# One buffer layout from the last output product to the end, half products two blocks a bank with split weights reused, and accumulators walked back and forth

## The chip, the cores and the metric

The kernel runs on one core of a Trainium2 chip. The metric is the device time of one execution in microseconds (us). Five engines run their own instruction streams: PE multiplies matrices (PEld is its loading of the stationary operand), DVE and ACT work on tiles, POOL here only starts DMAs, and SP starts most DMAs. Each of SP, POOL and ACT starts the DMAs that it is given in the order of its stream.

## The reference

One decoder layer on 512 tokens of width 2048, all in float32:

```python
mod = (silu(c) @ w_ada + b_ada).reshape(B, 6, D)
sh1, sc1, gt1, sh2, sc2, gt2 = ...
h = rmsnorm(x, g_norm_mix) * (1 + sc1) + sh1
proj = h @ w_in                      # q, k, v, xr, xg
mixed = concat([rmsnorm(stick_breaking_attention(q, k, v), g_attn_out),
                rmsnorm(rg_lru(conv(xr)) * gelu(xg), g_lru_out)])
x = x + gt1 * (mixed @ w_out)        # 2048 -> 2048
h = rmsnorm(x, g_norm_mlp) * (1 + sc2) + sh2
hid = square(relu(h @ w_mlp_in))     # 2048 -> 8192
x = x + gt2 * (hid @ w_mlp_out)      # 8192 -> 2048
return rmsnorm(x, g_norm_final)
```

## The kernel before

Channels lie on the partitions, tokens along the free axis; A and B are the first and the last 256 tokens. A float32 product is made of three matmuls (`mm3`): each operand is split into a rounded high half and the rest, and high x high, high x low and low x high are added in PSUM. For a weight tile ACT makes the high half (a copy, L207 or L911) and DVE the low half (a subtraction, `low`, L115).

The part that the change touches begins near 706 us, at the last of four output products (`mixed @ w_out`, 512 output channels each). It has these pieces:

- *The last output product*, `out_src(3)`: 16 blocks of 128 input channels; 256 tokens at a time (a half product of 192 matmuls of 128x256), half A and then half B. Each half loads and splits the 16 weight blocks of 256 KB afresh (tiles `wr`, `wh`, `wl`). `out_evac` adds the product to xT, which it loads then, and the sums of squares (L737). The result `x1` is stored to DRAM by 16 DMAs on SP.
- *Group 0 of mlp_in*, `in_src(0)`, again as two half products. Its operand comes from generators that run in the background, `norm3` with `prep_a` (tokens A) and `prep_b` (tokens B): a normalization, and the split of h. Every finished block is a tick, and a generator's `yield 1.0` says how many ticks it waits until its next piece. Between the halves the generator is drained and the stage changes.
- *Groups 1 to 15 of mlp_in*: 512 hidden channels each, by Strassen's seven products on 2 x 2 blocks (`strassen`). One of its steps, a set, loads one `raw` tile of weights (512 KB, L903), makes four sums of blocks on DVE (`ts`, L905, L912, L913), splits them (`w3` 768 columns and `w4` 1024 columns, L911 and L917) and issues 42 matmuls of 128x256 (L944 to L946). A group has eight sets and seven accumulators of one PSUM bank each, of eight banks. `combine` (L956 and on) makes four quarters of the seven; `sums()` made the sums of the activations ahead of group 1; `keep_parts` squares each group's result, splits it, forms four sums and stores it all to DRAM by POOL (`part`, `sum`, `p21`).
- *mlp_out*: 32 pairs (a pair is 256 hidden channels, half a group) times four groups n of 512 outputs, 124 sets by `strassen` and the rest, the last four pairs of n=3, as a plain product. Each set needs a pair's activations, five 256-KB loads on SP (`load_pair`, L985 and L988), whose sums are split three sets later (`arriving`, L994 and L115). 64 `a` tiles of 256 KB hold pairs, spills and results. The sets are walked in 18 parts (n, sets). When a part ends and its n is not finished, its seven accumulators are copied out (ACT L335 and DVE L337 in turn) and stored to DRAM by POOL (L1126); before a part whose n has been begun they are loaded by SP (`load_pre`, L1072, into seven `pre` tiles) and copied by ACT into PSUM (L934).
- *ada_late(GT2)*: the last modulation vector, 64 rows of 128x512 weights, each a load into `st` (256 KB, L1029) and a multiply with accumulation on DVE (L1040), one every 1.6 ticks in mlp_out.

Instructions are put in order by a scheduler that goes by the order of the program and by priorities (`tc.high_priority(offset=...)`: an offset moves the piece ahead by so much); after that each engine runs its list in order. Tiles come from rings: a tag with so many buffers; a writer waits until the last reader of the ring's oldest tile is done. Rings outside a stage last for the whole kernel (`BUFS`), those in `STAGES` lie over each other:

```python
    "front": {"x": 3, "tt": 5, "wr": 4, "wh": 3, "wl": 3, "n": 5},
    "mlp_in": {"raw": 3, "ts": 2, "w4": 6, "w3": 6},
    "mlp_out": {"raw": 3, "ts": 2, "w4": 4, "w3": 4, "pre": 7, "st": 2},
```

The walk of mlp_out:

```python
FROM = [0, 2, 3, 4]
parts = [(n, range(FROM[n])) for n in range(1, NO)]
parts += [(n, range(i + FROM[n], min(i + FROM[n] + 8, NP))) for i in range(0, NP, 8) for n in range(NO)]
```

Of the kernel before, what the change touches and what calls it, by code (L numbers as in the profile page):

```python
# [62 lines left out]
def hybrid_layer_kernel(  # L63
# [665 lines left out]
    def out_evac(bs, g, tok):  # L729
        for o in range(4):  # L730
# [6 lines left out]
            stt(out=t, in0=bs[o][:, tok], scalar=mod(GT1, k), in1=xr_[:, tok], op0=ALU.mult, op1=ALU.add)  # L737
# [558 lines left out]
```

## Time and profile before

| | |
|---|---|
| runs | 2165.39, 2159.66, 2163.75 us; median 2163.75 |
| profiled execution | 2159.86 us, span 2158.2 us |
| mean granted PE clock | 0.984 of full |
| PE busy in the span | 95% |
| DVE, ACT, POOL busy | 83%, 51%, 8% |
| DMA | 475.06 MB, mean 220 GB/s |

The profile is of one execution. A line number (L944) is that of the kernel before; a row gives line, engine, operation, tile written <- tile read, count and time. A wait is put down to the instruction whose end came last. PE's busy time counts modelled ends of matmuls, so a stretch where PE is busy all the time can still run at a slow clock; the granted clock stands beside it. What an engine other than PE waits for costs nothing by itself.

### The profile page before, as it was taken

How to read it: one execution, taken by the hardware profiler on the slowest of the kernel's cores; microseconds unless marked ns; L12 is line 12 of the kernel's file. 1: busy time of each engine (PE TensorE's matmuls, PEld its weight loads, DVE VectorE, ACT ScalarE, POOL GpSimd, SP SyncE). 2: the span in 40 equal slices, each digit the busy share in tenths (PEclk: the TensorE clock that was granted, in tenths of full speed). 3: DMA queues.
4: the chain of work that ended last, by engine and by line, in shares of the span. 5: the costliest groups of instructions: out<-in, count | busy, mean ns of one | idle time of the engine just before them, and what ended most of it. 6: DMA issues, size and time to landing. Idle time of an engine off the chain costs nothing.

```text
span 2158.2 us, 38620 instructions
## 1 busy us (share of the span) xinstructions
PE 2042.1 (95%) x14532; PEld 1907.9 (88%) x14532; DVE 1800.3 (83%) x3026; ACT 1107.8 (51%) x1657; POOL 180.2 (8%) x276
## 2 busy tenths in 40 slices
PE   7999999999999979999999999979999999999997
PEld 5779898778777868999999999979999999899996
DVE  6898775878888789998998988978888787877897
ACT  4433553885422575554544544554446445544452
POOL 0000000000000001121121121112001000100000
PEclk9999999999999999999999999989999999999999
DMA  8887644545779745565464555688768868777843
GB/s 287 281 292 239 202 146 139 164 146 181 234 254 317 252 143 179 165 199 167 150 202 157 167 186 165 191 324 304 259 217 316 304 232 287 254 274 260 309 144 113
DMA packets 225053, 475.06 MB, mean 220 GB/s; under 512 B 22497, under 2 KB 45153, under 8 KB 224866
## 3 DMA queue, kind: packets, MB, share of 16 engines
q1 hardware_dynamic: 201138, 400.63, 56.4%
q0 software_dynamic: 21280, 69.75, 8.9%
q8 instruction: 114, 1.87, 0.4%
q10 hardware_dynamic: 2448, 2.21, 0.3%
q14 instruction: 73, 0.60, 0.1%
HBM read 394.38 MB, written 78.12 MB: 219 GB/s over the span
## 4 chain that ended last, share of the span: by engine, by line
PE 35%; issue 26%; DMA 16%; DVE 13%; POOL 5%; ACT 3%; SPq 1%; POOLq 0%; DVEq 0%; ACTq 0%
DMA x<-in_w_adaT_dram 5%; PE ps_mm L222 3%; PE ps_mm L226 3%; PE ps_mm L225 3%; DVE w L115 3%; DMA raw<-in_w_mlp_out_dram 3%; POOL part L839 3%; PE ps_mm L946 3%; PE ps_mm L944 2%; PE ps_mm L945 2%; DMA st<-in_w_adaT_dram 2%; POOL sum L848 2%; DMA a<-sum 2%; PE ps_z L946 2%; PE ps_z L944 2%
## 5 line engine op out<-in xcount | busy, mean ns | idle before, releaser
L946 PE MATMUL ps_mm<-a,w 128*128 128x256 f32 x1704 | 483.4, 285 | 10.4 <-DVE w L115 9.9
L944 PE MATMUL ps_mm<-a,w 128*128 128x256 f32 x1704 | 482.9, 284 | 5.5 <-ACT w L911 5.3
L945 PE MATMUL ps_mm<-a,w 128*128 128x256 f32 x1704 | 481.2, 283 | 0.0
L911 ACT ACTIVATE w<-raw 128x768 fp32r<-128x768 f32 x244 | 205.5, 842 | 435.1 <-issue 124.9
L944 PE MATMUL ps_z<-a,w 128*128 128x256 f32 x1288 | 366.1, 284 | 19.9 <-ACT w L911 12.8
L946 PE MATMUL ps_z<-a,w 128*128 128x256 f32 x1288 | 366.5, 285 | 6.2 <-DVE w L115 6.2
L945 PE MATMUL ps_z<-a,w 128*128 128x256 f32 x1288 | 364.3, 283 | 0.0
L946 PEld LDWEIGHTS ps_mm<-a,w 128*128 128x128 f32 x1704 | 322.7, 190 | 15.4 <-DVE w L115 15.0
L944 PEld LDWEIGHTS ps_mm<-a,w 128*128 128x128 f32 x1704 | 324.0, 190 | 7.1 <-ACT w L911 6.1
L945 PEld LDWEIGHTS ps_mm<-a,w 128*128 128x128 f32 x1704 | 323.8, 190 | 0.0
L115 DVE TENSOR_TENSOR w<-raw,w 128x768 fp32r<-128x768 f32 (+1 forms) x262 | 244.5, 934 | 71.0 <-ACT w L911 67.0
L115 DVE TENSOR_TENSOR w<-ts,w 128x1024 fp32r<-128x1024 f32 x244 | 297.6, 1220 | 3.3 <-ACT w L917 3.1
L917 ACT ACTIVATE w<-ts 128x1024 fp32r<-128x1024 f32 x244 | 255.8, 1049 | 42.4 <-DVE ts L913 37.8
L944 PEld LDWEIGHTS ps_z<-a,w 128*128 128x128 f32 x1288 | 244.6, 190 | 22.3 <-ACT w L911 14.0
L946 PEld LDWEIGHTS ps_z<-a,w 128*128 128x128 f32 x1288 | 244.4, 190 | 9.6 <-DVE w L115 9.2
L181 DVE SCALAR_TENSOR_TENSOR x<-x,cb 128x1024 f32<-128x1024 f32 x160 | 195.5, 1227 | 64.0 <-DMA x<-in_w_adaT_dram 63.4
L945 PEld LDWEIGHTS ps_z<-a,w 128*128 128x128 f32 x1288 | 244.7, 190 | 0.0
L207 ACT ACTIVATE wh<-wr 128x512 fp32r<-128x512 f32 x232 | 142.9, 619 | 194.5 <-PE ps_mm L225 90.7
L905 DVE TENSOR_TENSOR ts<-raw 128x512 f32<-128x512 f32 x244 | 167.3, 687 | 69.7 <-DMA raw<-in_w_mlp_out_dram 59.5
L222 PE MATMUL ps_mm<-a,wh 128*128 128x512 f32 (+1 forms) x528 | 201.0, 381 | 8.7 <-DVE a L401 3.1
L226 PE MATMUL ps_mm<-a,wl 128*128 128x512 f32 (+1 forms) x528 | 200.0, 380 | 2.7 <-DVE wl L115 2.6
L115 DVE TENSOR_TENSOR wl<-wr,wh 128x512 fp32r<-128x512 f32 x232 | 158.5, 686 | 50.1 <-ACT wh L207 49.4
(293 smaller groups left out, 4134.7 us busy)
## 6 DMA issues: line engine op xcount, KB each, us to landing
x<-in_w_adaT_dram SPq DMA_DIRECT2D x160, 512.0 KB, 5.2
raw<-in_w_mlp_out_dram SPq DMA_DIRECT2D x124, 512.0 KB, 4.7
raw<-in_w_mlp_in_dram SPq DMA_DIRECT2D x120, 512.0 KB, 3.8
wr<-in_w_in_dram SPq DMA_DIRECT2D x160, 256.0 KB, 3.7
prod<-a POOLq DMA_DIRECT2D x98, 256.0 KB, 6.2
pre<-prod SPq DMA_DIRECT2D x98, 256.0 KB, 6.7
part<-a POOLq DMA_DIRECT2D x96, 256.0 KB, 3.6
a<-part SPq DMA_DIRECT2D x96, 256.0 KB, 6.6
```

What stands on the lines that cost most here:

```text
L115: tt(out=out, in0=full, in1=f32(high), op=ALU.subtract)
L181: stt(out=t, in0=t, scalar=1.0, in1=cb[q * n // 1024][:, o : o + n], op0=ALU.mult, op1=ALU.mult, accum_out=ga[:, q : q + 1],)
L207: act(h[:, :n], r[:, :n], AF.Copy)
L222: first = mm(out, wh, ah, start=start, stop=False, **kw)
L225: mm(out, wh, al, start=False, stop=False, **kw)
L226: mm(out, wl, ah, start=False, stop=stop, **kw)
L905: tt(out=t[:, : 2 * HT].rearrange("p (a b) -> p a b", a=2), in0=r[:, HT : 3 * HT].rearrange("p (a b) -> p a b", a=2), in1=r[:, q_(0)].unsq ...
L911: act(h, r[:, HT:], AF.Copy)
L917: act(h, t, AF.Copy)
L944: mm(out, wh[:, blk(i)], ah, start=st, stop=False, **kw)
L945: mm(out, wh[:, blk(i)], al, start=False, stop=False, **kw)
L946: mm(out, wl[:, blk(i)], ah, start=False, stop=j == js[-1], **kw)
```

## The change

1. *Stages.* `n` is a ring of the whole kernel; the stage `front` ends before the last output product, and one stage `mlp` follows to the end: `ts` 2, `raw` 3, `w4` 5, `w3` 6. The rings `pre` and `st` are gone.
2. *Half products.* `half_product` puts two blocks of outputs into one PSUM bank, so a half product takes two banks. It keeps the split weights of eight blocks of `out_src(3)` and ten of `in_src(0)` from half A and uses them in half B, which walks backwards. That is 18 loads and splits less. xT of the last product comes in two loads of 512 KB into `ts` tiles; the stores of x1 go from SP's queue to POOL's. `sums()` runs beside group 0 and group 1, in reverse order of j, and so do group 1's sets.
3. *ada_late* starts with group 2 of mlp_in, a row every 2.6 ticks, loaded three rows ahead: 47 rows run in mlp_in (tile `n`) and 17 in mlp_out (tile `a`).
4. *The last two groups* (pairs 28 to 31) stay in SBUF (`hold_parts`), and the order of the pairs is 28, 29, 0 to 3, 30, 31, 4 to 27. Each other pair is loaded four to seven sets before its first use and split two sets before it, by a table.
5. *The walk* goes back and forth: 13 parts, 9 spills and 9 reloads of seven accumulators instead of 14. Of a reload, five loads go out on POOL's queue at the part before, and two on ACT's queue at the border, all into `n` tiles.
6. *The tail's* kept weights lie in `w4` and `w3` instead of `w4` and `a`.

```diff
-    "front": {"x": 3, "tt": 5, "wr": 4, "wh": 3, "wl": 3, "n": 5},
-    "mlp_in": {"raw": 3, "ts": 2, "w4": 6, "w3": 6},
-    "mlp_out": {"raw": 3, "ts": 2, "w4": 4, "w3": 4, "pre": 7, "st": 2},
+    "front": {"x": 3, "tt": 5, "wr": 4, "wh": 3, "wl": 3},
+    "mlp": {"ts": 2, "raw": 3, "w4": 5, "w3": 6},
...
-    def norm3(tok, prep):
-        yield 1.8
-        rnorm([acc1], D, "o", tok, r2)
+    def norm3(tok, prep, ptag):
+        yield 5.0
+        rnorm([acc1], D, ptag, tok, r2)
...
+    def half_product(bs, src, operand, ks, held, keep={}):
+        for k in ks:
+            wh, wl = held[k] if k in held else weights(src(k), keep.get(k, "w4"))
+            if k in keep:
+                held[k] = wh, wl
+            ah, al = operand(k)
+            for o, out in enumerate(halves(bs)):
+                mm3(out, wh[:, blk(o)], wl[:, blk(o)], ah, al, k == ks[0] and o % 2 == 0, k == ks[-1], ...)
+            tick()
...
-    product(ba, out_src(3), mx, order, A)
-    out_evac(ba, 3, A)
...
+    stage("mlp")
+    half_product(b2, out_src(3), mixed_half(A), order, held, dict(zip(order[8:], ["w3"] * 3 + ["w4"] * 5)))
+    out_evac(halves(b2), 3, A, x3)
+    b2 = [bank("mm") for _ in range(2)]
+    for k in range(12):
+        nc.gpsimd.dma_start(x1D[k], x1[k])
+    bg.add(norm3(A, prep_a, "o"))
+    half_product(b2, out_src(3), mixed_half(B), order[::-1], held)
...
+    bg.add(norm3(B, prep_b, "z"), sums())
+    half_product(b2, in_src(0), h2_half(A), PAIRED, held, dict(zip(PAIRED[6:], ["w3"] * 3 + ["ts"] * 2 + ["w4"] * 5)))
...
+    half_product(b2, in_src(0), h2_half(B), BACK, held)
...
         if pre:
+            n, ts = pre
             with tc.high_priority(offset=SETE):
-                for b, t in zip(bs, pre):
+                for b, t in zip(bs, ts):
+                    act(b, t, AF.Copy)
+                for b, t in zip(bs[5:], load_pre(n, (5, 6), nc.scalar)):
                     act(b, t, AF.Copy)
...
+        if g == 2:
+            bg2.add(ada_late(GT2))
...
+        bg.add((keep_parts if g < NG - 2 else hold_parts)(g, *rs))
...
-    bg.drain()
-    stage("mlp_out")
+    parts = [
+        (0, range(8)), (1, range(8)), (2, range(8)), (3, range(16)), (2, range(8, 16)), (1, range(8, 16)), (0, range(8, 24)),
+        (1, range(16, 24)), (2, range(16, 24)), (3, range(16, 28)), (0, range(24, NP)), (1, range(24, NP)), (2, range(24, NP)),
+    ]
+    ORDER = [28, 29, 0, 1, 2, 3, 30, 31] + list(range(4, 28))
+            todo.setdefault(use - 7 - q % 8 + q % 8 * 3 // 2, []).append((load_pair, p))
+            todo.setdefault(use - 2, []).append((split_pair, p))
...
-    def load_pre(n):
-        ts = [T("pre") for _ in range(7)]
-        for t, d in zip(ts, prodD[n]):
-            nc.sync.dma_start(t, d)
+    def load_pre(n, js, queue=nc.gpsimd):
+        ts = [T("n") for _ in js]
+        for t, j in zip(ts, js):
+            queue.dma_start(t, prodD[n][j])
         return ts
...
-                return load_pre(left[0])
+                return left[0], load_pre(left[0], range(5))
...
-    tags = ["w4"] * 2 + ["a"] * 6
+    tags = ["w4"] * 3 + ["w3"] * 2 + ["w4"] * 2 + ["w3"]
```

How the instructions stand on the engines, at three places. First, SP at the start of the last output product, before (x is the last ada's tile, wr a weight block, n a block of xT, x_0 a block of x1 in DRAM):

```order
L177 DMA x_6273<-in_w_adaT_dram 128x1024
L199 DMA wr_6570<-in_w_out_dram 128x512
L199 DMA wr_6588<-in_w_out_dram 128x512
L199 DMA wr_6606<-in_w_out_dram 128x512
L735 DMA n_6476<-in_xT_dram 128x512
L199 DMA wr_6624<-in_w_out_dram 128x512
L735 DMA n_6482<-in_xT_dram 128x512
L735 DMA n_6488<-in_xT_dram 128x512
L199 DMA wr_6642<-in_w_out_dram 128x512
```

And in the changed kernel:

```order
L174 DMA x_6272<-in_w_adaT_dram 128x1024
L735 DMA n_6475<-in_xT_dram 128x512
L735 DMA n_6481<-in_xT_dram 128x512
L735 DMA n_6487<-in_xT_dram 128x512
L735 DMA n_6493<-in_xT_dram 128x512
L196 DMA raw_6579<-in_w_out_dram 128x512
L196 DMA raw_6596<-in_w_out_dram 128x512
L196 DMA raw_6613<-in_w_out_dram 128x512
L924 DMA ts_6573<-in_xT_dram 128x2x512
L924 DMA ts_6574<-in_xT_dram 128x2x512
L196 DMA raw_6630<-in_w_out_dram 128x512
```

The weights of the last product now go into three `raw` tiles of the new stage, behind the four loads of xT of the product before; the first of them waits for DVE's last use of the x tile that lay there.

Second, SP at the start of mlp_out, before (a<-part and a<-sum are a pair's loads, raw a set's weights):

```order
L985 DMA a_15759<-part_6518 128x512
L988 DMA a_15763<-sum_6534 128x512
L988 DMA a_15764<-sum_6534 128x512
L903 DMA raw_15876<-in_w_mlp_out_dram 128x2x512
L903 DMA raw_15942<-in_w_mlp_out_dram 128x2x512
L903 DMA raw_16036<-in_w_mlp_out_dram 128x2x512
L1029 DMA st_15938<-in_w_adaT_dram 128x512
```

And in the changed kernel:

```order
L959 DMA raw_15655<-in_w_mlp_in_dram 128x2x512
L959 DMA raw_15775<-in_w_mlp_out_dram 128x2x512
L959 DMA raw_15859<-in_w_mlp_out_dram 128x2x512
L1042 DMA a_15512<-part_6514 128x512
L1042 DMA a_15513<-part_6514 128x512
L1042 DMA a_15514<-part_6514 128x512
L1045 DMA a_15518<-sum_6530 128x512
L1045 DMA a_15519<-sum_6530 128x512
```

Before, the first weights of mlp_out stand behind all forty loads of eight pairs; now they stand behind the last weights of mlp_in and ahead of the first pair's loads (pair 0).

Third, a border between two parts of mlp_out. Before, on SP (pre<-prod is a reload):

```order
L903 DMA raw_17135<-in_w_mlp_out_dram 128x2x512
L903 DMA raw_17191<-in_w_mlp_out_dram 128x2x512
L903 DMA raw_17252<-in_w_mlp_out_dram 128x2x512
L1072 DMA pre_17053<-prod_1_15852 128x512
L1072 DMA pre_17054<-prod_2_15853 128x512
L1072 DMA pre_17055<-prod_3_15854 128x512
L1072 DMA pre_17056<-prod_4_15855 128x512
L1072 DMA pre_17057<-prod_5_15856 128x512
L1072 DMA pre_17058<-prod_6_15857 128x512
L985 DMA a_17122<-part_6520 128x512
L903 DMA raw_17318<-in_w_mlp_out_dram 128x2x512
```

In the changed kernel, on ACT (L332 copies an old accumulator out, L991 and L993 bring a new one into PSUM, L967 and L973 split weights, and the sixth and seventh accumulator are prod_5 and prod_6):

```order
L332 ACTIVATE a_18877<-ps_mm_18391 128x512
L991 ACTIVATE ps_mm_18899<-n_18410 128x512
L332 ACTIVATE a_18883<-ps_o_18393 128x512
L1140 DMA n_18911<-prod_6_15749 128x512
L991 ACTIVATE ps_mm_18900<-n_18411 128x512
L991 ACTIVATE ps_o_18901<-n_18412 128x512
L991 ACTIVATE ps_z_18902<-n_18413 128x512
L332 ACTIVATE a_18889<-ps_z_18395 128x512
L967 ACTIVATE w_3185_19043<-raw_19039 128x768
L993 ACTIVATE ps_z_18903<-n_18910 128x512
L332 ACTIVATE a_18895<-ps_mm_18397 128x512
L993 ACTIVATE ps_z_18904<-n_18911 128x512
```

SP has no reload left between its weights; the seventh accumulator's load is on ACT, eight instructions ahead of the copy that needs it.

More of the change, by code (lines that the diff above doesn't have):

```diff
@@ L864, in of @@
             if tok.start == 0:
-                return Half(raw_h[j][:, q_(c)], A), Half(raw_l[j][:, q_(c)], A)
-            t = (half2 if c else other)[j]
-            return Half(t[:, q_(0)], B), Half(t[:, q_(1)], B)
+                return raw_h[j][:, q_(c)], raw_l[j][:, q_(c)]
+            side = half2 if c else other
+            while j not in side:
+                assert bg.next()
+            return side[j][:, q_(0)], side[j][:, q_(1)]
         return of
+    stage("mlp")
     r2 = T("n")
@@ L878, in hybrid_layer_kernel @@
+    b2 = [bank("z") for _ in range(2)]
+    held = {}
+    half_product(b2, out_src(3), mixed_half(A), order, held, dict(zip(order[8:], ["w3"] * 3 + ["w4"] * 5)))
[5 more added lines that the diff above has]
+    half_product(b2, out_src(3), mixed_half(B), order[::-1], held)
     bg.drain()
     with tc.high_priority(offset=URGENT):
-        out_evac(bb, 3, B)
@@ L881, in hybrid_layer_kernel @@
-    for k in range(NK):
-        nc.sync.dma_start(x1D[k], x1[k])
-    ba = [bank("z") for _ in range(3)] + [bank("mm")]
-    bg.add(norm3(B, prep_b))
-    product(ba, in_src(0), h2_half(A), PAIRED, A)
-    r11, r12 = relu_half(ba, A)
-    bb = [bank("mm") for _ in range(3)] + [bank("o")]
-    bg.drain()
-    stage("mlp_in")
-    bg.add(sums())
-    product(bb, in_src(0), h2_half(B), PAIRED, B, held={}, keep={k: "w4" for k in PAIRED}, urgent=450)
-    r21, r22 = relu_half(bb, B)
-    bg.drain()
@@ L894, in hybrid_layer_kernel @@
-    bg.add(keep_parts(0, r11, r12, r22, r21))
+        out_evac(halves(b2), 3, B, x3)
+    for k in range(12, NK):
+        nc.gpsimd.dma_start(x1D[k], x1[k])
+    b2 = [bank("z"), bank("mm")]
+    bg.add(norm3(B, prep_b, "z"), sums())
+    held = {}
+    half_product(b2, in_src(0), h2_half(A), PAIRED, held, dict(zip(PAIRED[6:], ["w3"] * 3 + ["ts"] * 2 + ["w4"] * 5)))
+    r11, r12 = relu_half(b2)
+    b2 = [bank("o"), bank("mm")]
+    half_product(b2, in_src(0), h2_half(B), BACK, held)
+    r21, r22 = relu_half(b2)
@@ L969, in acts_in @@
     def acts_in(j):
+        while j not in sums_:
+            assert bg.next()
         rh, rl, (s12, s34) = raw_h[j], raw_l[j], sums_[j]
@@ L1009, in hybrid_layer_kernel @@
[L1009 to L1023 removed]
+        loaded_s[p] = ss
@@ new lines, in load_pair, with split_pair, acts_out @@
+        pairs[p] = {n: (t[:, q_(0)], t[:, q_(1)]) for n, t in zip(("11", "12", "22"), ts)}
+    def split_pair(p):
+        for i, t in enumerate(loaded_s.pop(p)):
+            h = T("a", F32R)
+            act(h, f32(t), AF.Copy)
+            low(t, f32(t), h)
+            for n in range(2):
+                pairs[p][f"s{2 * i + n + 1}"] = h[:, q_(n)], t[:, q_(n)]
+    def acts_out(q):
+        p = ORDER[q]
+        while p not in pairs:
+            assert bg.next()
+        return pairs[p]
+    NO, NP = 4, DFF // 256
```

189 lines of the change are left out of this document (104 added, 85 removed).

## The prediction

> **What bounds the kernel now.** I read the page first (lines 1 and 4: TensorE, PE below, is busy for 95% of the span), then a table by stretch, then the waits of PE, then SP's own queue at one part boundary. The change begins near 706 us, at the last output product, so the table starts there. Its columns are the stretch, its length, busy time and count of PE, PEld, DVE, ACT and POOL, the granted clock, the DMA share and GB/s.
>
> ```profile
> PE 2042.1 (95%) x14532; PEld 1907.9 (88%) x14532; DVE 1800.3 (83%) x3026; ACT 1107.8 (51%) x1657; POOL 180.2 (8%) x276
> ...
> 706.00:823.90 117.90, 98.28 (x773) 94.66 (x772) 96.44 (x199) 79.78 (x162) 0.00 (x0) 0.96 0.62 195
> 823.90:871.20 47.30, 43.22 (x336) 42.00 (x337) 45.37 (x73) 23.98 (x35) 7.20 (x10) 0.93 0.56 177
> 871.20:1429.00 557.80, 557.80 (x4703) 557.80 (x4702) 498.72 (x747) 288.63 (x397) 98.06 (x142) 1.00 0.58 185
> 1429.00:1491.00 62.00, 47.17 (x342) 45.64 (x341) 53.47 (x95) 31.80 (x46) 15.85 (x26) 0.83 0.83 289
> 1491.00:2114.00 623.00, 597.90 (x4874) 586.82 (x4873) 515.63 (x854) 321.54 (x447) 47.36 (x88) 0.99 0.74 259
> 2114.00:2158.20 44.20, 29.55 (x215) 27.01 (x213) 30.41 (x69) 10.45 (x22) 0.00 (x0) 0.90 0.34 113
> ```
>
> The third row is the pace: PE never idle, 557.80 us / 4703 matmuls = 0.1186 us each (128x256). Busy time hides what a row loses to a slow clock, so I use length minus count times 0.1186 as the loss: half products 26.2 us (117.9 - 773 x 0.1186), first full group 7.4, later groups 0, the border from mlp_in to mlp_out 21.4, mlp_out 44.9, tail 18.7. PE issues the same 14506 matmuls after the change, so it can win these losses only, and the first, second, fourth and fifth are the ones it touches: 99.9 us at most.
>
> Who is late, for PE (706 to 2114) and then for all (1491 to 2114) and SP's queue:
>
> ```profile
> PE ps_z L944 <- ACT w L911: 12.8, 5, 9.2
> PE ps_mm L222 <- ACT w L207: 11.0, 2, 10.7
> PE ps_mm L946 <- DVE w L115: 9.9, 16, 2.4
> ...
> PE ps_mm L944 <- ACT w L911: 5.3, 4, 1.9
> PE ps_mm L222 <- DVE a L737: 2.8, 1, 2.8
> ...
> DVE ts L905 <- DMA raw<-in_w_mlp_out_dram: 57.9, 21, 5.2
> ...
> SPq L903 <- DVE w L115: 255.5, 93, 6.7
> ...
> SPq L1072 <- ACT ps_mm L934: 17.6, 24, 1.4
> ```
>
> L944 to L946 are the three matmuls of a Strassen product, L911 and L115 the split of their weights into a high half (ACT) and a low one (DVE), L905 sums made of fresh weights; L903 loads weights, L1072 reloads an accumulator. PE waits for splits, and DVE for the weights' landing (21 waits, 57.9 us). SP's first row is harmless (the buffer is not yet free); in the second SP stands at a reload until ACT has copied the one before into PSUM. In order on one queue, the next weights stand behind it:
>
> ```profile
> 1708.48 4.54 SPq L1072 DMA_DIRECT2D pre<-prod  x6
> ...
> 1719.11 0.38 SPq L903 DMA_DIRECT2D raw<-in_w_mlp_out_dram  x1
> ...
> 1727.99 0.38 SPq L903 DMA_DIRECT2D raw<-in_w_mlp_out_dram  x1
> ...
> 1721.00:1731.00 10.00, 7.63 (x54) 7.03 (x53) 6.23 (x11) 4.51 (x6) 0.00 (x0) 0.91 0.86 317
> ```
>
> Weights go out at 1719 and then not for 8.9 us; a set lasts 42 x 0.1186 = 4.98 us, and PE is busy 7.63 of the 10 us there.
>
> **Half products: 26.2 us becomes about 13.** Four halves of 192 matmuls (22.8 us each by the pace). Rows of this stretch:
>
> ```profile
> 797.00:823.90 26.90, 25.65 (x192) 24.49 (x192) 23.27 (x49) 15.45 (x27) 0.00 (x0) 0.93 0.57 170
> ...
> 755.00:765.00 10.00, 7.02 (x57) 6.61 (x57) 8.91 (x20) 8.15 (x20) 0.00 (x0) 1.00 0.58 174
> 785.00:797.00 12.00, 1.32 (x10) 1.11 (x9) 10.39 (x27) 11.54 (x28) 0.00 (x0) 0.73 0.00 0
> ...
> 703.03 1.16 DVE x L181 x2
> ...
> 721.85 6.87 DMA wr<-in_w_out_dram
> ...
> 761.86 2.32 DMA n<-in_xT_dram
> ...
> 802.65 4.40 DMA raw<-in_w_mlp_in_dram
> 807.15 0.64 ACT w L207
> ...
> 809.47 3.09 DMA raw<-in_w_mlp_in_dram
> ...
> wr<-in_w_out_dram SPq DMA_DIRECT2D x33, 256.0 KB, 4.1
> ```
>
> What goes: the hole of 785 to 797 (10.7 us of wait for ACT in the PE waits; no DMA in it, since the next stage's weights wait for a drain and ACT is busy with prep_b), because there is no stage border there now, and 10 of the 16 split blocks are held. The 2.8 us behind out_evac (L737), which itself stands behind a 2.32-us load of xT, goes because xT is loaded early and banks are not reused at once. What comes: the stage now opens before the last output product, and its first raw buffer lies over x of the last ada instruction, which ends at 703.03 + 1.16 = 704.2. The first weights go out there, land 4.1 later, and are split in 0.64: 708.9, so PE stands from about 706, 2.9 us (0 if PE still has work, 5.7 with a landing of 6.87); I take 3. Then three raw buffers feed 16 blocks: the loop of load, ACT and DVE took from 802.65 to 809.47, 6.8 us for three blocks against 36 x 0.1186 = 4.27 of PE; but the whole half that ran that way (first row) lost 26.9 - 22.8 = 4.1. I take 4.1, between 0 and 5.3 x 2.55 = 13.6. The other three halves, with eight and ten blocks already split, I give 2 each. Sum 13, between 5 and 24. Eighteen loads and splits less (18 x 256 KB) are what hides the rest; the 16 stores of x1, moved from SP to POOL, have nobody behind them but the stores of group 0.
>
> The hole has a second price, the clock: the 10-us one granted 0.73, while the row 755 to 765, which holds the 2.8-us wait, granted 1.00. [...]
>
> **Group 1: 7.4 becomes 4.** DVE is busy 45.37 of 47.30 there, so it is DVE's stage. sums() now runs in the reverse order beside it, and hands over blocks as they are needed; I halve the loss (0 to 10).
>
> **Groups 2 to 15: 0 becomes 2.** 64 rows of the late modulation move; 47 of them from mlp_out into this stage:
>
> ```profile
> L1040 DVE SCALAR_TENSOR_TENSOR st<-st,cb x64: 678/684/694, 1464.6 to 2004.2; 128x512 f32<-128x512 f32 x64
> L1040 DVE DVE_READ_ACCUMULATOR st<-st,cb x64: 77/81/84, 1465.2 to 2004.8; 128x1 f32 x64
> ```
>
> 47 x (0.684 + 0.081) = 36.0 us of DVE into 557.8 us with 498.72 busy: 96%. The cover is DVE's idle 59 us; without it the whole 36 falls on PE. Weights' second half also has five buffers instead of six. I take 2, between 0 and 36. Their loads (47 x 256 KB, 12 MB) lie in a DMA share of 0.58.
>
> **The border: 21.4 becomes 4.** The chain of waits there:
>
> ```profile
> 1420.65 0.69 POOL sum L848
> ...
> 1423.25 5.87 DMA sum<-a
> ...
> 1429.54 8.25 DMA raw<-in_w_mlp_out_dram
> ```
>
> SP stood at a reload of a sum that group 15 had only just stored, the first weights of mlp_out behind it; PE waited 9.2 (the longest of L944) and the clock fell to 0.83. Now the last two groups stay in SBUF, and the first weights go out among earlier pairs' loads. Left: a pair's five 256-KB loads ahead of a raw, 1.31 MB at 289 GB/s = 4.5 us, once. I take 4, between 0 and 21.4.
>
> **mlp_out: 44.9 becomes 14.** Reloads of seven accumulators fall from 14 (98 loads) to 9 (63), stores likewise; five of each seven go out on POOL's queue eight sets early, two on ACT's queue at the boundary, none on SP. 44.9 / 14 = 3.2 us each before.
>
> ```profile
> L934 ACT ACTIVATE ps_mm<-pre x50: 578/594/605, 1502.8 to 2092.3; 128x512 f32<-128x512 f32 x50
> ...
> prod<-a POOLq DMA_DIRECT2D x98, 256.0 KB, 6.2
> pre<-prod SPq DMA_DIRECT2D x98, 256.0 KB, 6.7
> ```
>
> What stays is ACT's burst of four copies out and seven in (11 x 0.594 = 6.5 us, in which splits wait). Floor: one restore on the path, 9 x 0.594 = 5; ceiling: no cheaper than before, 9 x 3.2 = 29. I take the mean of PE's short waits for ACT (5.3 / 4 = 1.3), 9 x 1.3 = 11.9, and one wait of 2.4 for DVE at the first spill, where DVE's copies need tiles that the first stores still hold: 14. The sixth and seventh accumulator are the narrow place. The last load goes out on ACT about 3.1 us before the new part begins (PE frees the first bank 36 matmuls = 4.3 us before, then a copy and a restore), lands 6.7 later, and its bank is needed 36 matmuls after the start, at 4.3: just in time. POOL's loads stand behind its stores, but have 8 x 4.98 = 40 us.
>
> **Tail: 18.7 stays**; its kept weights only change buffers.
>
> **Sum.** Gains 13.2 + 3.4 - 2 + 17.4 + 30.9 = 62.9. The profiled execution took 2159.86 (span 2158.2), so 2097; the median of the runs, 2163.75, lies 3.9 above it, and I add half of that: 2099. With all lower ends (5, 0, 0, 0, 5) the gain is 89.9, so 2070 on the profiled run; not all come together, and I take 2077 as the low end.
>
> **Rivals.**
> (1) DVE fills up in mlp_in. For: 96% is close, and PE's most frequent wait is for DVE. Against: the row shows PE without one lost microsecond at 89%. Price: 34 more than I counted, 2133.
> (2) The reloads' landing, not SP's order, sets the loss. For: the DMA share at the boundary is 0.86 at 317 GB/s, so bytes may be what is late, and they are the same bytes on any queue. Against: SP itself waits at L1072, and a third of the reloads go. Price: 29 instead of 14, and half products at 22 instead of 13 since their landings are as crowded: 2099 + 15 + 9 = 2123. [...]
> (3) Nothing won: the losses only move. If the leaner buffers (five instead of six) and the added rows let weights come no faster than one set in 5.55 us, 0.57 above PE's 4.98, the 112 sets of groups 2 to 15 lose 64 us and the gain is gone: 2099 - 2 + 64 = 2161. Against: DVE's 498.72 + 36.0 over 112 sets is 4.77.
> (4) Slower: the last reload on ACT's queue lands late at every boundary and blocks ACT, which is in order, with all splits behind it. Beyond a landing of 6.7 each extra us costs one at each of 9 boundaries; it eats the 63 us at 6.7 + 7 = 13.7, and at 15 the time is 2099 + 9 x 8.3 = 2174. For: the rows above show landings of 8.25 beside other loads. Against: that was 512 KB; this is half, and SP's bytes there are fewer than before.
>
> **How the numbers follow.** My forecast 0.60, (1) 0.13, (2) 0.15, (3) 0.05, (4) 0.07. A change under 0.3% (6.5 us) can't be told from none here. Faster: 0.60 + 0.13 + 0.15 = 0.88; (3) counts as same, 0.05; (4) as slower, 0.07. The range 2077 to 2135 holds the forecast and the first two rivals but for their edges.
>
> **What would show it.** Right: from 871 us on to the end of mlp_in a row with PE at its length and DVE near 96%; no reload on SP's queue and no weights held there for over 6 us; no hole over 5 us between 706 and 871; a border with clock near 1.00; PE waits for ACT's L911 (its line moves) under 15 us in mlp_out. Wrong: PE waiting for DVE in mlp_in (1), DVE waiting for weights' DMA as long as before (2), ACT waiting for n<-prod for several us at each boundary (4), or a first hole near 706 much over 6 us.

## The result and the profile after

The changed kernel takes 2096.6 us (median of four runs, 2089.3 to 2100.6) against 2161.7 (2158.8 to 2165.4): ratio 0.969, 95% interval 0.966 to 0.973. The forecast was 2099. One of the four executions of ada_out below took 3263.4 us at a mean clock of 0.558; the time given for that kernel is of the other three. The profiled execution took 2092.94 us, span 2091.2 at a mean clock of 0.993. The same table as before, by stretch (length, busy time and count of PE, PEld, DVE, ACT and POOL, granted clock, DMA share, GB/s): half products, group 1, groups 2 to 15, border, mlp_out, tail.

```profile
706.00:810.00 104.00, 97.74 (x775) 94.53 (x774) 79.20 (x165) 66.67 (x138) 3.93 (x8) 0.98 0.49 157
810.00:859.10 49.10, 43.58 (x339) 43.07 (x338) 43.69 (x79) 24.94 (x35) 5.51 (x8) 0.93 0.51 166
859.10:1420.10 561.00, 559.66 (x4706) 558.56 (x4705) 529.66 (x883) 303.35 (x400) 92.72 (x136) 1.00 0.61 196
1420.10:1461.40 41.30, 40.82 (x338) 40.31 (x337) 41.16 (x65) 27.77 (x41) 0.56 (x1) 1.00 0.49 169
1461.40:2048.00 586.60, 581.30 (x4874) 580.35 (x4873) 479.87 (x745) 300.83 (x397) 60.05 (x111) 1.00 0.65 229
2048.00:2091.20 43.20, 28.66 (x214) 26.46 (x213) 29.80 (x67) 10.01 (x22) 0.00 (x0) 0.90 0.46 155
```

Loss is again length less count times 0.1186 us:

| stretch | before | forecast | after |
|---|---|---|---|
| half products | 26.2 | 13 | 12.1 |
| group 1 | 7.4 | 4 | 8.9 |
| groups 2 to 15 | 0 | 2 | 2.9 |
| border | 21.4 | 4 | 1.2 |
| mlp_out | 44.9 | 14 | 8.5 |
| tail | 18.7 | 18.7 | 17.8 |
| sum | 118.6 | 55.7 | 51.4 |

118.6 - 51.4 = 67.2, the 67.0 us between the two spans. What PE waits for now (700 to 2048 us), and ACT and DVE in mlp_out at late tiles:

```profile
PE ps_z L1005 <- DVE w L112: 6.9, 4, 4.1
...
ACT a L1052 <- DMA a<-sum: 7.5, 4, 2.6
...
DVE a L1104 <- DMA a<-in_w_adaT_dram: 11.1, 3, 8.7
```

L1003 to L1005 are the set's matmuls now, L112 the low half, L1052 the split of a pair's sums, L1104 a late row. The longest single hole of mlp_out is a late row: its load landed after 10.84 us, DVE stood at it for 8.67, and PE behind it (the chain of waits, then DVE's timeline); from 1555 to 1565 us PE is busy for 6.75 of 10 us, at a granted clock of 0.83.

```profile
1547.65 10.84 DMA a<-in_w_adaT_dram
...
1558.59 0.69 DVE L1104 SCALAR_TENSOR_TENSOR a<-a,cb 128x512 f32<-128x512 f32 x1 [8.67 <-DMA a<-in_w_adaT_dram]
```

### The profile page after: what moved, and what is told of

Its sections match the earlier page's. It is cut to its first block, busy times and chain, and to the rows that moved or that the text cites. A ratio compares the mean times of both kernels' runs of the same rounds, so it can differ in the third digit from the quotient of the medians.

```text
span 2091.2 us, 38025 instructions
## 1 busy us (share of the span) xinstructions
PE 2016.1 (96%) x14532; PEld 1892.5 (90%) x14532; DVE 1765.3 (84%) x2993; ACT 1084.4 (52%) x1580; POOL 179.5 (9%) x282
## 4 chain that ended last, share of the span: by engine, by line
PE 49%; DVE 3%; DMA 2%; issue 1%; ACT 0%; SPq 0%; DVEq 0%; ACTq 0%
PE ps_mm L1004 8%; PE ps_mm L1003 8%; PE ps_mm L1005 8%; PE ps_z L1004 6%; PE ps_z L1003 6%; PE ps_z L1005 6%; PE ps_o L1005 2%; PE ps_o L1004 2%; PE ps_o L1003 2%; DVE w L112 1%; DMA raw<-in_w_mlp_out_dram 1%; DMA a<-in_w_adaT_dram 1%; DMA a<-x 1%; DMA a<-sum 0%; DVE a L1180 0%
## 5 line engine op out<-in xcount | busy, mean ns | idle before, releaser
L1005 PE MATMUL ps_mm<-a,w 128*128 128x256 f32 x1696 | 476.6, 282 | 1.1 <-DVE w L112 1.1
L1003 PE MATMUL ps_mm<-a,w 128*128 128x256 f32 x1696 | 477.1, 282 | 0.5 <-DVE a L1016 0.5
L1004 PE MATMUL ps_mm<-a,w 128*128 128x256 f32 x1696 | 477.2, 282 | 0.0
L967 ACT ACTIVATE w<-raw 128x768 fp32r<-128x768 f32 x244 | 205.0, 841 | 330.8 <-PE ps_mm L1004 145.9
L1005 PE MATMUL ps_z<-a,w 128*128 128x256 f32 x1304 | 368.7, 283 | 7.0 <-DVE w L112 6.9
L112 DVE TENSOR_TENSOR w<-ts,w 128x1024 fp32r<-128x1024 f32 x244 | 297.7, 1220 | 89.5 <-PE ps_mm L1004 41.0
L1003 PE MATMUL ps_z<-a,w 128*128 128x256 f32 x1304 | 368.5, 283 | 0.5 <-DVE a L1019 0.5
L973 ACT ACTIVATE w<-ts 128x1024 fp32r<-128x1024 f32 x244 | 258.3, 1059 | 152.1 <-DVE ts L969 134.2
L1005 PEld LDWEIGHTS ps_mm<-a,w 128*128 128x128 f32 x1696 | 319.3, 189 | 1.4 <-DVE w L112 1.4
L1003 PEld LDWEIGHTS ps_mm<-a,w 128*128 128x128 f32 x1696 | 319.4, 188 | 0.8 <-issue 0.7
L1004 PEld LDWEIGHTS ps_mm<-a,w 128*128 128x128 f32 x1696 | 319.6, 189 | 0.1
L112 DVE TENSOR_TENSOR w<-raw,w 128x768 fp32r<-128x768 f32 (+1 forms) x296 | 267.3, 904 | 42.7 <-ACT w L204 27.8
L1005 PEld LDWEIGHTS ps_z<-a,w 128*128 128x128 f32 x1304 | 246.8, 189 | 8.3 <-DVE w L112 8.2
L1003 PEld LDWEIGHTS ps_z<-a,w 128*128 128x128 f32 x1304 | 246.9, 189 | 0.9 <-issue 0.7
L204 ACT ACTIVATE wh<-wr 128x512 fp32r<-128x512 f32 (+1 forms) x184 | 113.1, 618 | 171.3 <-PE ps_mm L222 74.3
L223 PE MATMUL ps_mm<-a,wl 128*128 128x512 f32 x448 | 178.0, 398 | 7.2 <-DVE wl L112 7.1
L219 PE MATMUL ps_mm<-a,wh 128*128 128x512 f32 x448 | 178.0, 397 | 4.0 <-DVE a L380 3.1
L222 PE MATMUL ps_mm<-a,wh 128*128 128x512 f32 x448 | 176.8, 395 | 0.0
```

The lines of the kernel that those rows point to most:

```text
L112: tt(out=out, in0=full, in1=f32(high), op=ALU.subtract)
L204: act(h[:, :n], r[:, :n], AF.Copy)
L219: first = mm(out, wh, ah, start=start, stop=False, **kw)
L222: mm(out, wh, al, start=False, stop=False, **kw)
L223: mm(out, wl, ah, start=False, stop=stop, **kw)
L967: act(h, r[:, HT:], AF.Copy)
```

## The experiments

Each kernel is profiled once and timed against the kernel before. The part ahead of 706 us is the same work everywhere, but its end lies between 706 and 719 us in these profiles, so small differences of total time say less than losses; "mlp_out with border" below is the stretch from the last set of group 15 to the last set of mlp_out: 66.6 us lost before (689.5 - 5252 x 0.1186), 10.0 after.

```profile
1424.50:2114.00 689.50, 649.58 (x5252) 636.96 (x5251) 571.24 (x951) 353.33 (x492) 64.58 (x116) 0.98 0.75 262
...
1415.10:2048.00 632.90, 627.12 (x5252) 625.66 (x5251) 524.88 (x815) 330.94 (x440) 60.61 (x112) 1.00 0.64 227
```

**The queue of the reloads.** Two kernels: in the changed one all reloads go back to SP; in the one before they go to POOL.

```diff
-    def load_pre(n, js, queue=nc.gpsimd):
+    def load_pre(n, js, queue=nc.sync):
-                for b, t in zip(bs[5:], load_pre(n, (5, 6), nc.scalar)):
+                for b, t in zip(bs[5:], load_pre(n, (5, 6))):
```

> The changed kernel with all 63 reloads of accumulators started on SP's queue, at the same places of the program (five a part ahead, two at the border); nothing else differs. Theory Q (it was SP's order that cost): each of the 9 borders loses 2 to 3 us again, mlp_out's loss (length less count times 0.1186 us) goes from 8.5 to 25 to 35 us, and the kernel is 15 to 27 us slower than the changed one, near 2115 us. Theory L (landings and bytes cost, the queue is indifferent): loss within 5 us of 8.5, time within 6 us of the changed kernel.

```diff
 def load_pre(n):                      # kernel before
-            nc.sync.dma_start(t, d)
+            nc.gpsimd.dma_start(t, d)
```

> The kernel before with one edit: its 98 reloads are started on POOL's queue instead of SP's. Theory Q: mlp_out's loss falls from 44.9 to 15 to 25 us, the time by 20 to 30 us to about 2135. Theory L: the loss stays within 8 us of 44.9 and the time within 8 us of 2161.7.

The stretch of mlp_out with border in each, first the changed kernel with SP, then the one before with POOL, and there ACT's wait for a pair's sums and DVE's for fresh weights:

```profile
1414.60:2044.00 629.40, 625.39 (x5252) 624.20 (x5251) 525.54 (x815) 328.88 (x440) 36.12 (x67) 1.00 0.66 228
...
1427.20:2150.50 723.30, 662.95 (x5252) 653.46 (x5251) 572.94 (x951) 353.76 (x493) 118.50 (x214) 0.94 0.71 250
...
ACT a L994 <- DMA a<-sum: 74.5, 15, 10.1
...
DVE ts L905 <- DMA raw<-in_w_mlp_out_dram: 80.7, 23, 8.7
```

With SP the loss is 6.5 us (10.0 with POOL and ACT) and the time 2093.9 (ratio 0.967, 0.964 to 0.970): in the changed kernel the queue is indifferent. With POOL the kernel before loses 100.4 and takes 2194.3 us, 1.4% more (1.011 to 1.017; 2163.6 for the kernel before in the same session, 31 us). Theory Q falls, and with it the reason of the prediction for mlp_out. Theory L has the first kernel right and the second wrong: the queue did not only fail to help there, it hurt. A border of that kernel shows what is full:

```profile
1592.00:1596.00 4.00, 4.00 (x36) 4.00 (x36) 2.55 (x3) 3.48 (x6) 2.36 (x5) 1.00 1.03 412
1596.00:1600.00 4.00, 4.00 (x36) 4.00 (x35) 3.08 (x5) 1.14 (x2) 1.65 (x3) 1.00 0.97 358
1600.00:1604.00 4.00, 4.00 (x36) 4.00 (x35) 0.00 (x0) 0.00 (x0) 0.00 (x0) 1.00 1.04 390
1604.00:1608.00 4.00, 2.10 (x18) 1.89 (x16) 2.13 (x4) 2.00 (x4) 0.00 (x0) 1.00 0.99 365
...
1605.89 1.36 ACT L994 ACTIVATE a<-a 128x512 fp32r<-128x512 f32 x2 [8.76 <-DMA a<-sum]
```

For 16 us the DMA engines are at 0.97 to 1.04, with stores, reloads, the loads of a new pair and weights all in them. ACT stands for 8.76 us at the split of that pair's sums, DVE does nothing for four of them, and the splits of weights are queued behind on ACT. PE runs on for 12 us from what is split, then stops. ACT's wait for sums is hardly longer over the whole stretch than before (74.5 us against 69.4), DVE's wait for weights is (80.7 against 59.5, 23 waits each). Why the kernel loses 34 us more was not tested: at this border POOL starts six of the seven reloads no sooner after the first store than SP did, only the last one (9.9 us after it, SP 15.5).

**The split of a pair's sums, later.** If it is ACT standing there, a later split should free it.

```diff
-        arriving.append([3, later_split])    # kernel before
+        arriving.append([7, later_split])
```

> The kernel before with one number changed: a pair's sums are split on ACT seven sets after their load instead of three. New theory S (at a border the DMA engines are full, and ACT stands, in order, at the split of a pair's sums, L994, 15 times and 69.4 us in all, with the weights' splits behind it): those waits fall under 15 us, mlp_out's loss from 44.9 to 12 to 25 us, the time by 20 to 33 us to about 2135. Rival (the bytes at the border set the loss, whoever waits for them): the loss stays above 35 us and the time within 8 us of before.

2153.0 us, ratio 0.993 (0.990 to 0.996): some 13 us better, not 20 to 33; in its profile, the slowest of its runs, the loss is 63.3 (686.1 - 5251 x 0.1186), and ACT's wait is 40.6 us, not under 15. Behind the border PE's waits for ACT nearly go (7.7 us before, 2.2 now), those for DVE stay (16.0 and 16.9), and DVE waits for weights as before (54.3 us in 17, against 57.9 in 21). So ACT's standing at this split is a part of the cost. That the full DMA engines are another, by weights that land late, is argued from DVE's wait and not shown by a run of its own.

```profile
ACT a L994 <- DMA a<-sum: 40.6, 9, 8.7
...
DVE ts L905 <- DMA raw<-in_w_mlp_out_dram: 54.3, 17, 4.8
```

**The rows of the late modulation.** Three kernels: all 64 rows in mlp_in, all in mlp_out (both in the new layout), and all in mlp_in of the kernel before.

```diff
-    pace[0] = 2.6
+    pace[0] = 1.7                       # ada_in
-        if g == 2:
-            bg2.add(ada_late(GT2))
+    bg2.add(ada_late(GT2))              # ada_out: at the start of mlp_out, pace 1.6
-            t = T("st")
+            t = T("a")                  # before_ada_in, started at g == 2, pace 1.7
```

> The changed kernel with the late modulation's rows at 1.7 ticks instead of 2.6, so that all 64 lie in mlp_in and none in mlp_out. My theory: DVE in groups 2 to 15 goes from 530 to 543 of 561 us (97%) and still loses nothing there (under 4 us); the 4.95-us hole in mlp_out, where DVE stood 8.67 us at a late row, is gone; 3 to 6 us faster than the changed kernel. Rival (DVE full): mlp_in loses 10 to 15 us and the kernel is 5 to 10 us slower.

> The changed kernel with all 64 rows of the late modulation back in mlp_out, every 1.6 ticks as before, in the new layout. My theory: DVE in groups 2 to 15 falls to about 495 us of 558 and the loss there stays under 3; mlp_out gets 36 us more of DVE (516 of 590) and more waits for late rows, in order on DVE: loss 15 to 25 us instead of 8.5, the kernel 7 to 16 us slower than the changed one. Rival: the rows' place is worth nothing, within 4 us.

> The kernel before with one part of the change alone: the 64 rows of the late modulation run in mlp_in (from group 2 on, every 1.7 ticks, one row loaded ahead, in a tiles), none in mlp_out. Theory D (in mlp_out the rows cost twice, as 64 x 256 KB in full DMA engines and as in-order waits of DVE): mlp_out's loss falls from 44.9 to 18 to 30 us, mlp_in loses under 4, time 14 to 26 us below before, near 2142. Rival (reloads and pairs at the border set the loss): loss above 38 us, time within 7 us of before.

Rows: groups 2 to 15 and mlp_out with border of ada_in; mlp_out with border of ada_out and its DVE's wait; the same two stretches of before_ada_in.

```profile
859.50:1414.90 555.40, 554.38 (x4665) 553.56 (x4664) 536.38 (x924) 301.89 (x397) 92.81 (x136) 1.00 0.63 204
1414.90:2042.10 627.20, 625.17 (x5251) 623.67 (x5250) 514.78 (x766) 329.81 (x440) 60.63 (x112) 1.00 0.63 221
...
1414.20:2071.50 657.30, 636.92 (x5252) 631.53 (x5251) 550.48 (x927) 328.32 (x440) 60.65 (x112) 0.99 0.69 236
...
DVE a L1104 <- DMA a<-in_w_adaT_dram: 50.5, 23, 7.7
...
879.80:1442.70 562.90, 558.02 (x4664) 554.75 (x4663) 526.86 (x901) 289.20 (x396) 95.92 (x140) 1.00 0.65 208
1442.70:2110.90 668.20, 641.60 (x5252) 634.34 (x5251) 538.88 (x793) 353.07 (x494) 64.90 (x117) 0.98 0.70 246
```

ada_in: DVE is 97% full in mlp_in (536.4 of 555.4) and PE loses 2.1 us there; mlp_out with border loses 4.4. 2090.4 us, ratio 0.966 (0.963 to 0.969): the best of all kernels here, though its interval overlaps the changed kernel's. ada_out: 2116.1 us (0.975 to 0.983), loss 34.4, more than the 15 to 25 expected, and DVE stands 50.5 us, 23 times, at rows that are late. The two differ by 30 us of loss (26 by the median times), in little but the place of the rows (their pace is 1.7 or 1.6 ticks): as many rows at 3 rows' notice cost PE next to nothing in mlp_in, where the DMA share is 0.63, and half a microsecond of loss each among the borders of mlp_out. What their loads and what their work on DVE cost there was not told apart. In the kernel before the same move takes 21.3 us off mlp_out (66.6 to 45.3), gives back 9.7 in mlp_in, where its loads have one row's notice, and 11 us remain by the medians (ratio 0.9956, 0.9942 to 0.9970): less than theory D expected and more than its rival. ACT's wait for pairs' sums hardly changes there (68.8 us in 13 waits, 69.4 in 15 before), so most of the 21.3 us do not hang on it.

**The last groups through DRAM.** Group 15 is stored and loaded again, and read by the first sets.

```diff
+        bg.add((hold_parts if g == NG - 2 else keep_parts)(g, *rs))
+    bg.drain()
+    for p in (30, 31):
+        load_pair(p)
+        split_pair(p)
-    ORDER = [28, 29, 0, 1, 2, 3, 30, 31] + list(range(4, 28))
+    ORDER = [30, 31, 0, 1, 2, 3, 28, 29] + list(range(4, 28))
```

> The changed kernel with group 15 (pairs 30 and 31) sent through DRAM again and read by the first two sets of mlp_out, after a drain; group 14 stays in SBUF. My theory of the border: the first pair's loads wait for the stores, weights behind them: the border's loss goes from 1.2 to 10 to 20 us, time 9 to 19 us above the changed kernel. Rival: the border's gain came from opening no new stage; then under 4 us.

```profile
PE ps_z L1003 <- DMA a<-part: 16.9, 1, 16.9
...
1424.50:1493.20 68.70, 50.39 (x381) 49.11 (x379) 51.57 (x86) 31.67 (x46) 9.32 (x15) 0.83 0.64 206
```

2122.1 us (0.978 to 0.983). The border loses 68.7 - 381 x 0.1186 = 23.5 us, as much as before the change (21.4); PE waits 16.9 at once for a pair that comes back from DRAM, and the clock is 0.83. The theory holds, at a price above its range: 22.3 us more at the border, 25.5 of time.

**No reuse of split weights.**

```diff
             wh, wl = held[k] if k in held else weights(src(k), keep.get(k, "w4"))
-            if k in keep:
-                held[k] = wh, wl
```

> The changed kernel without holding split weights between half products: 18 more loads of 256 KB and 18 more splits; the banks, the layout and the walk stay. My theory: the loop of three raw buffers feeds the B halves too, so each of them loses about 4 us: the loss from 706 us to the first Strassen set goes from 12 to 18 to 24 us, the kernel 6 to 12 us slower than the changed one. Rival (the gain came from the stage border that went): under 3 us.

```profile
712.90:823.70 110.80, 102.88 (x772) 96.15 (x772) 83.27 (x169) 72.13 (x148) 2.15 (x4) 0.98 0.58 180
```

2107.0 us, 10.4 above the changed kernel. From its first half matmul the half products lose 19.2 us (110.8 - 772 x 0.1186; 100.8 - 91.6 = 9.2 in the changed kernel) and group 1 12.3 (52.1 - 336 x 0.1186; 8.9). The half products lose 10 us more, within the 6 to 12 that the theory gave.

**The walk.** First in blocks of four pairs, so with 15 reloads; then the old walk with 14; then the old walk with pairs loaded later. All three have their rows in mlp_in and are compared with ada_in (4.4 us lost, 2090.4 us).

```diff
     parts = [                                                         # blocks4_in
+        (0, range(8)), (1, range(8)), (2, range(8)), (3, range(12)), (2, range(8, 12)), (1, range(8, 12)), (0, range(8, 16)),
+        (1, range(12, 16)), (2, range(12, 16)), (3, range(12, 20)), ...
+    FROM = [0, 2, 3, 4]                                               # old_walk_in
+    parts = [(n, range(FROM[n])) for n in range(1, NO)]
+    parts += [(n, range(i + FROM[n], min(i + FROM[n] + 8, NP))) for i in range(0, NP, 8) for n in range(NO)]
-            todo.setdefault(use - 7 - q % 8 + q % 8 * 3 // 2, [])...  # old_walk_late, beside the old walk
+            todo.setdefault(use - 4, [])...
-            todo.setdefault(use - 2, [])...
+            todo.setdefault(use - 1, [])...
```

> The changed kernel walked in blocks of four pairs instead of eight: 15 reloads of seven accumulators instead of 9 (19 parts instead of 13), with all late rows in mlp_in as in the run ada_in (2090.4 us, mlp_out's loss 8.3), which it is compared with. New theory (a reload costs PE next to nothing where weights and pairs are not late): at most 0.7 us for each of 6 more, loss under 13, time within 5 us of ada_in. Rival (a reload costs about 3.2 us as counted in the prediction): loss 25 to 30, time 17 to 22 us above ada_in.

> The changed kernel with the walk of before (18 parts, 14 reloads instead of 9), with all late rows in mlp_in; compared with the run ada_in (2090.4 us, mlp_out's loss 8.3). Theory (a reload is covered when parts are eight sets long; the 3.3 us that each of the six more cost in blocks of four came from parts too short for the loads to land): loss under 16, time at most 8 us above ada_in. Rival (a reload costs 3.2 us wherever it is): loss 24 or more, time 14 to 20 us above ada_in.

> The run old_walk_in (walk of before in the new layout, 2145.7 us, mlp_out's loss 60) with a pair's five loads four sets before its first use instead of four to seven, and its split one set before instead of two: with this walk new pairs are first used in the last two to four sets of a part, so their loads leave the first sets behind a border, where spills and reloads fill the DMA engines. Same number of loads, reloads and sets. Theory B (what the new walk took away is the meeting of pair loads with spills and reloads at a border, where ACT and DVE then stand in order at late tiles): mlp_out's loss falls from 60 to 25 to 42 us, ACT's wait for a<-sum (66.8 us in 24) by more than half, time 12 to 30 us below old_walk_in. Rival (the 14 reloads themselves): loss stays above 50, time within 8 us.

```profile
1413.50:2062.40 648.90, 632.11 (x5252) 628.69 (x5251) 523.72 (x785) 364.16 (x506) 100.00 (x184) 1.00 0.70 247
...
1416.90:2095.90 679.00, 643.80 (x5252) 640.05 (x5251) 524.75 (x781) 356.74 (x496) 93.16 (x172) 0.97 0.66 232
...
1418.20:2084.80 666.60, 638.28 (x5252) 634.25 (x5251) 525.36 (x781) 357.92 (x496) 93.12 (x172) 0.98 0.67 238
```

| kernel | reloads | time, us | mlp_out with border, lost |
|---|---|---|---|
| ada_in | 9 | 2090.4 | 4.4 |
| blocks4_in | 15 | 2110.3 | 26.0 |
| old_walk_in | 14 | 2145.7 | 56.1 |
| old_walk_late | 14 | 2133.8 | 43.7 |

The expectations give 8.3 and 60 us of loss where this table has 4.4 and 56.1: both are 3.9 higher, so the differences are the same.

In blocks of four each of six more reloads costs 3.3 us of time: the rival's price, not the theory's, though with parts of four sets. At L993 PE waits there for the sixth and seventh accumulator (5.5, 3.1 and 3.1 us at copies from `n` tiles by ACT). But the old walk has one reload fewer than that and loses 30 us more; at 55 us above ada_in it lies far above what the theory (8) and its rival (20) allowed, so the number of reloads is not the whole. A border of it, against one of ada_in:

```profile
1558.00:1564.00 6.00, 6.00 (x53) 6.00 (x52) 4.07 (x6) 2.03 (x3) 1.86 (x5) 1.00 0.97 357
1564.00:1570.00 6.00, 6.00 (x53) 6.00 (x52) 2.41 (x4) 2.32 (x3) 0.94 (x2) 1.00 1.04 411
1570.00:1576.00 6.00, 2.88 (x25) 2.67 (x23) 2.67 (x4) 3.27 (x5) 0.00 (x0) 0.99 0.48 178
...
1565.02 0.60 ACT L991 ACTIVATE ps_mm<-n 128x512 f32<-128x512 f32 x1 [4.39 <-DMA n<-prod]
1572.30 0.63 ACT L1052 ACTIVATE a<-a 128x512 fp32r<-128x512 f32 x1 [4.96 <-DMA a<-sum]
...
1618.00:1624.00 6.00, 6.00 (x53) 6.00 (x52) 5.63 (x10) 5.66 (x10) 4.40 (x9) 1.00 0.93 310
1624.00:1630.00 6.00, 6.00 (x53) 6.00 (x53) 3.41 (x5) 2.78 (x5) 1.56 (x3) 1.00 1.01 362
1630.00:1636.00 6.00, 6.00 (x53) 6.00 (x52) 4.76 (x9) 2.65 (x4) 0.00 (x0) 1.00 0.77 288
...
1627.13 0.60 ACT L991 ACTIVATE ps_mm<-n 128x512 f32<-128x512 f32 x1 [2.95 <-DMA n<-prod]
```

Both fill the DMA engines for about 12 us. In the old walk a part's new pairs are first used in its last sets, so their loads fall on the border; ACT stands 4.39 us for a reload and then 4.96 for a pair's sums, and PE loses 3 of 6 us. In the new walk a border inside a block brings no new pair; ACT stands 2.95 us for a reload there and at no pair's sums, and PE does not notice. Over mlp_out ACT waits 66.8 us (24 times) for pairs' sums with the old walk (the row below), 7.5 (4 times) in the changed kernel, 69.4 (15 times) in the kernel before.

```profile
ACT a L1052 <- DMA a<-sum: 66.8, 24, 6.2
```

Moving the loads up to three sets later, and the splits one, took off 12 of 56 us and 12.0 us of time, at the lower edge of theory B in time (12 to 30) and short of it in loss (18 to 35 off), but more than its rival gave (8 us of time); ACT's wait for sums, which was to fall by more than half, did not fall, it is 71.5 us in 29. So the place of the pairs' loads matters, but how the other 39 us of the old walk divide between pairs that are still late and the reloads themselves stays open.

Nor are the 52 us between ada_in and old_walk_in what the new walk saved the kernel before. before_ada_in has the same old walk and its rows in mlp_in too, but its reloads on SP. The stretch of mlp_out behind the border in both, before_ada_in first:

```profile
1507.00:2110.90 603.90, 593.05 (x4890) 587.27 (x4889) 484.37 (x708) 321.12 (x447) 47.21 (x88) 0.99 0.68 242
...
1461.50:2096.00 634.50, 603.24 (x4921) 600.52 (x4920) 481.72 (x716) 328.23 (x452) 82.92 (x153) 0.97 0.65 232
```

The kernel before loses 24.0 us there (603.9 - 4890 x 0.1186; 44.9 with its rows), the changed layout with the same walk 50.9 (634.5 - 4921 x 0.1186). So the rest of the change makes the old walk worse, and with the rows out of its way the new walk had at most 24 us to win. The old walk in the changed layout with its reloads on SP was not run, though POOL's queue cost the kernel before 34 us of loss; nor were the longer rings of split weights (five `w4` and six `w3` instead of four each) tested alone.

**A try at more.** The subtractions of `sums()` on POOL.

```diff
-            tt(out=s12[:, q_(0)], ...)                          # and three more
+            nc.gpsimd.tensor_tensor(out=s12[:, q_(0)], ...)
```

> A try at a faster version: the run ada_in with the 32 subtractions and additions of sums() on POOL instead of DVE (256 columns each, 0.34 us apart on DVE, 11 us in all). In the changed kernel group 1 of mlp_in loses 8 to 9 us with DVE busy 15.00 of 15 us there. Theory: the loss of group 1 falls to 1 to 4 us, time 4 to 7 us below ada_in, near 2085. Rival (POOL is slower and the sums come late, or POOL's and DVE's accesses hinder each other): no gain or up to 6 us slower.

```profile
708.40:819.50 111.10, 99.34 (x772) 95.99 (x773) 86.20 (x150) 66.38 (x137) 28.01 (x29) 0.95 0.45 143
```

2098.6 us (0.969 to 0.973), 8 above ada_in: half products lose 19.5 from their first matmul (9.8 in ada_in by the same count) and group 1 11.0 (51.2 - 339 x 0.1186; 7.8 in ada_in). DVE is no less busy: 86.2 us in the row above, 75.8 in ada_in, though it has ten instructions fewer. The rival holds, at 2 us more than its range; which of its two reasons it was, no run shows.

## Why the prediction was right, and where

**mlp_out: the size right, the reason wrong.** I read 44.9 us as 14 reloads of 3.2 us each, held up by SP's order, and took 14 for what would be left; 8.5 were left. The row that I built on, SP's 17.6 us behind L1072, was real, but taking the reloads off SP bought nothing: with all of them on SP the changed kernel is as fast, and on POOL they did not help the kernel before. Rival (2), that bytes and landings set the loss on whatever queue, is what the runs of the changed kernel show of the queue, and the step that failed is "the next weights stand behind it". That the gain of mlp_out came near the forecast in spite of this (36.4 us, 30.9 forecast) is luck. At the very place that I quoted, where no weights went out from 1719 to 1728, the kernel before shows another engine (its stretch, then ACT's and DVE's timelines, then ACT's wait from 1491 to 2114):

```profile
1718.00:1724.00 6.00, 6.00 (x53) 6.00 (x52) 1.99 (x4) 0.00 (x0) 0.00 (x0) 1.00 1.05 400
...
1725.60 0.63 ACT L994 ACTIVATE a<-a 128x512 fp32r<-128x512 f32 x1 [8.60 <-DMA a<-sum]
...
1727.00 0.96 DVE L115 TENSOR_TENSOR w<-raw,w 128x768 fp32r<-128x768 f32 x1
...
ACT a L994 <- DMA a<-sum: 69.4, 15, 9.0
```

The DMA engines were full, ACT did nothing for 8.60 us but stand at a pair's sums, the splits of weights behind it, and so raw buffers did not come free: SP's next weights wait 3.8 us, until 1727.99, for the low half of 1727.00, the last reader of their buffer; what stood ahead of them on SP did not set that time. The sum of it, 69.4 us in 15 waits of ACT at L994, was in the trace of before, about one wait for each border, and I passed it over since ACT is busy only half the time. It is not a measure of the loss: before_ada_in waits as long and loses 21.3 us less, and old_walk_late waits longer than old_walk_in and loses 12 less. What shows in the kernel before is that the rows alone held 21 of the 44.9 us; how the other 24 divide between ACT's standing, late weights and the rest is open. The two runs with the queue changed show no gain from starting the reloads elsewhere than on SP: the changed kernel takes 2093.9 us with all of them on SP and 2096.6 with POOL and ACT, and in the kernel before the move to POOL cost 31 us (2194.3 against 2163.6).

**The rows' move was priced on one side only.** I counted 36 us of DVE added to mlp_in, at 2 us of PE. That was right: 2.9 lost, DVE at 529.7 of 561. What they cost in mlp_out was left in the sum of "reloads". In the new layout that is 24 us: loss 34.4 with all rows there, 10.0 with 17, 4.4 with none.

**Border and half products** came as said. With group 15 sent through DRAM again the border loses 23.5 instead of 1.2, and without the reuse the half products lose 10 us more. The first hole came too, a wait of 2.58 us against 2.9 forecast, but it was not the load that ended last:

```profile
708.03 0.63 ACT L300 ACTIVATE n<-a 128x512 f32<-128x512 f32 x1 [0.63 <-DVE a L737]
708.57 0.61 ACT L204 ACTIVATE w<-raw 128x512 fp32r<-128x512 f32 x1
...
709.23 0.39 PE L219 MATMUL ps_z<-a,w 128*128 128x256 f32 x1 [2.58 <-ACT w L204]
709.20:713.20 4.00, 3.10 (x15) 2.90 (x16) 2.78 (x5) 1.26 (x2) 0.00 (x0) 0.64 1.02 367
```

The split L204 starts without a wait of its own, behind ACT's sums of squares of the product before, so x's buffer, for which SP's load did wait 4.0 us, did not set the hole's length: the load went out at 703.91 and landed some 3.0 us later, 1.7 before its split. The clock behind the hole was 0.64 for 4 us, where in the kernel before the 4 us behind the wait of 2.81 us at out_evac (764.9 to 768.9, 33 matmuls) were granted 1.00. That is the second price weighed there; what sets the clock was not tested.

**Group 1** was the wrong term: 8.9 instead of 4, no better than before. sums() is still there as a burst: DVE is busy 15.00 of 15 us in the row below, PE 9.88, and the third set alone loses 6.7 us. The halving was a guess with no row behind it.

```profile
815.00:830.00 15.00, 9.88 (x81) 9.47 (x80) 15.00 (x34) 8.72 (x13) 0.00 (x0) 0.99 0.27 77
```

Rival (1) is refuted: with DVE at 97% groups 2 to 15 lost 2.1 us. Rival (4) cost most with parts of four sets (PE stood 11.7 us at the sixth and seventh accumulators). Its sign did appear in the changed kernel, where ACT stood at late reloads, though at the first five (L991): 23.7 us in 8 waits, the longest 4.4, for which PE never waited itself. The sign of rival (2) did not: DVE's wait for weights, 57.9 us before, is 3.2 in 4. (PE's matmuls are 14532 in both profiles, not 14506; no sum uses that number.) In the sum, mlp_out and the border were 8 us better than said and group 1 was 5 worse.

## What to carry to other kernels

Before a stall is put down to an issuing queue, look at each in-order engine for the late tile it stands at, and at what is queued behind it: an engine that is half idle can still be the one that stops the others (ACT, busy 51% before, stood 8.60 us at one pair's sums, the splits of weights behind it). At two borders with the DMA engines full for about 12 us, PE lost nothing in ada_in, where ACT stood 2.95 us at a late reload, and 3 of 6 us in old_walk_in, where ACT stood 4.39 us at a reload and 4.96 more at a pair's sums; so move small, regular loads (rows, pairs) to stretches with a free DMA share (0.63 in mlp_in of ada_in), and keep them off the moments of spill and reload. Parts that each remove such a meeting don't add up: undone alone (rows, group 15, walk) they cost 24, 25 and 52 us of mlp_out and border, together they had saved 57.

## What the runs showed of the hardware that was not expected

With the clock granted in full and PE never idle, 40 us hold 340 matmuls in the changed kernel (first row) and 335 in keep15 (second row), all of the same form; in most such stretches it is 339 and 336, 1% fewer. In keep15 it is 335 or 336 in all five such stretches read from 1500 to 1900 us; no_reuse has 340 from 1520 to 1560 and 336 from 1600 to 1640, behind a stall. Over mlp_out's 620 us 1% would be 6 us, and it counts as loss here: of keep15's 25 us some 5 are this pace, as an estimate (1% of the 530 us behind its border, if the pace is the same all along). Whether it is also why runs of one kernel lie 10 us apart can't be said from one profile of each. What sets the pace wasn't tested.

```profile
1620.00:1660.00 40.00, 40.00 (x340) 40.00 (x339) 31.28 (x49) 20.54 (x27) 6.50 (x12) 1.00 0.59 212
...
1620.00:1660.00 40.00, 40.00 (x335) 40.00 (x335) 38.32 (x63) 24.11 (x35) 4.75 (x9) 1.00 0.71 229
```
